# Six channel groups instead of three in a ConvFFN, with the down projection moved between the halves of the up projection

## The chip, the cores and the metric

The kernel runs on one core of one Trainium2 chip. A core has five engines that run side by side, each through its own instructions in order: TensorE (PE in the profile, its weight loads PEld) multiplies matrices into PSUM, VectorE (DVE) and ScalarE (ACT) work elementwise, GpSimd (POOL) does a few small things here, and SyncE (SP) issues the DMA transfers. PSUM has eight banks of 128 x 512 float32.

The metric is the device time of one execution in microseconds (us). The kernel before takes 1051.03 us, the median of three runs (1050.93 to 1052.33).

## The reference

Two layers of an encoder over 512 positions and 1024 channels, in float32. Each layer has a mixing part (a Fourier group and windowed attention, side by side, joined by `w_o`) and a ConvFFN. Cut to what matters:

```python
for l in range(2):
    h = rmsnorm(x, norm1[l])
    p = h @ w_in[l]                       # 1024 -> 512 Fourier | 512 q | 128 k | 128 v
    y_f = real(fft2(p[:, :512])) @ w_f + b_f
    y_a = windowed_gqa(rope(norm(q)), rope(norm(k)), v, sink)   # |i - j| <= 128
    x = x + concat(rmsnorm(y_f), rmsnorm(y_a)) @ w_o[l]
    h = rmsnorm(x, norm2[l])
    up = dwconv_centred(h @ w_up[l], conv_w[l], conv_b[l])      # 1024 -> 5632, 3 taps over positions
    gate, val = up[:, :2816], up[:, 2816:]
    x = x + (silu(gate) * val) @ w_down[l]                      # 2816 -> 1024
```

## The kernel before

**Layout.** Channels lie on the partitions, positions along the free axis: `x` is eight tiles of 128 x 512. The 2816 inner channels of the ConvFFN are 22 tiles of gate and 22 of value; a *pair* `fi` is gate tile `fi` and value tile `fi`.

**Precision.** Most products are made of two-part numbers. `split` (L100) makes the parts: ScalarE copies the rounded high part (`act`, L91, recorded as L92), VectorE subtracts it for the low part (`tt`, L94, recorded as L95). `mm3` (L116) multiplies in three passes, recorded as L122, L123 and L124. Weights arrive by DMA in a `wraw` tile of 128 x 1024 (three buffers, `wload`, L129) and are split into `whi` and `wlo` chunks of up to 512 columns (five buffers each, `wsplit`, L134).

**A pair with eight products** (`up_eight`, L428): for each of its two halves eight input tiles x three passes of 512 columns, 48 matmuls in all; four weight chunks are split; VectorE takes each half out of PSUM with the factor `rb2` of the norm.

**A pair with seven products** (`up_seven`, L440) treats the two halves and the two halves of the positions as a two-by-two block matrix and makes seven products of half the width in place of eight: 7 x 4 x 3 = 84 matmuls of 256 columns. In exchange VectorE forms four sums of weights, seven chunks are split, and the products are added up in more and shorter steps. It uses both `tp` banks of PSUM and one of the others. The combinations of the input that it needs (the T operands) are made once a layer by `seven_h` (L416), into sixteen tiles from `h_rooms` (L403). The fourth T product, which belongs to the second half alone, comes after the first half has been handed on. `SEVEN` (L37) names these pairs: four in the first layer, six in the second.

**After each half** `conv` (L476) applies three taps: one ScalarE instruction and two on VectorE (`stt`, L97, recorded as L98). After both, Silu, the product and a split give the pair's input `gu` to the down projection, in `slab` or `pT` tiles.

**Groups.** `GROUPS` (L36) cuts the 22 pairs into three groups of 8, 7 and 7. After a group's pairs come its eight down rows: for each of the eight tiles of `x`, one PSUM bank sums the group's products with `w_down`, and VectorE adds it to `x`. In the first layer's last group each row is followed by the square sums and the split of the next layer's norm (`norm_tile`, L335).

**Presplit.** During the first layer's ConvFFN, `presplit` (L153) splits the second layer's other weights into parts and stores them to HBM (`kept`), in 44 pieces. A piece is one ScalarE and one VectorE instruction and two stores; loads go into `m4` tiles, one job ahead. `next(ahead)` does a piece. Until now the first three `m4` tiles of `h_rooms` were also taken from those five buffers.

**Order.** The text of the program gives priorities; a scheduler with a model of the engines' times fixes each engine's order when the program is built. Instructions can therefore stand some way from where the text has them. At run time each engine keeps its order and waits where a result is late.

**First layer's Fourier stages.** In the first layer these run in plain float32 (L120). Each stage makes three PSUM tiles of even columns (`pe`) and one of odd ones (`po`), and `stage_out` (L714) copies them out with ScalarE.

The functions that the diff touches, and what calls them:

Of the kernel before, what the change touches and what calls it, by code (L numbers as in the profile page):

```python
# [12 lines left out]
ALU = mybir.AluOpType  # L13
# [22 lines left out]
GROUPS = [(0, 8), (8, 7), (15, 7)]  # L36
SEVEN = ((9, 12, 16, 19), (9, 11, 13, 16, 18, 20))  # L37


def encoder_kernel(tc, t):  # L40
# [445 lines left out]
    for l in range(L):  # L486
# [200 lines left out]
        for kk in range(KT // 2):  # L687
            if not l:
                wu = load_wu(l, kk)
            for k in (2 * kk, 2 * kk + 1):  # L690
# [7 lines left out]
                for m in range(3):  # L698
                    mm3(pee[m][:, :258], [z[:, m * P:(m + 1) * P] for z in h], we, st, sp_)
                for m in range(2):  # L700
                    mm3(poo[:, m * 256:(m + 1) * 256], [z[:, 256 + m * P:384 + m * P] for z in h], wo,
                        st and m == 0, sp_, skip_group_check=True)
# [11 lines left out]
        def stage_out(pe, po, scale, turned=False):  # L714

            tiles = []
            if not l:
                two = temp(1024, "slab")
            for m in range(2):
                a = halves(pair("slab")) if l else [two[:, m * 512:(m + 1) * 512]]  # L720
                put([z[:, :257] for z in a], pe[m][:, :257], scale)
                put([z[:, 257:] for z in a], po[:, m * 256 + 1:(m + 1) * 256], scale)
                tiles.append(a)
            return tiles, tail_out(pe, scale, turned)
# [3 lines left out]
        for stage in range(2):  # L728
            pe = [psum(), psum(), psum("sc")]
            po = psum()  # L730
            for m in range(3):
# [10 lines left out]
            for m in range(2):  # L742
                for i in range(2):
                    a, b = (ue, tabs) if stage == 0 else (tabs, ue)
                    mm3(po[:, m * 256:(m + 1) * 256], [z[:, 256 + m * P:384 + m * P] for z in a[i]],
                        [z[:, 256:512] for z in b[i]], m == 0 and i == 0, i == 1, skip_group_check=True)
# [77 lines left out]
        ts = []  # L824
        for f0, nf in GROUPS:
            gu = []
            for fi in range(f0, f0 + nf):
                ys_ = []
                n = fi - f0
# [129 lines left out]
```

## Time and profile before

| | |
|---|---|
| median of 3 runs | 1051.03 us |
| profiled execution, its own time | 1051.79 us |
| its span, first to last instruction | 1050.0 us |
| TensorE busy | 1032.8 us, 98% |
| VectorE busy | 797.3 us, 76% |
| ScalarE busy | 531.5 us, 51% |
| DMA | 140.1 MB, 41.4% of sixteen engines |
| mean granted TensorE clock | 0.998 |

A row of a timeline has the start in us from the beginning of the span, the duration in us, engine, line, operation, output <- inputs, shapes and how many instructions are merged; behind them, in brackets, how long the engine was idle before and what ended it. A row of a group has the count behind an x, then busy us and mean ns of one, then the idle time ahead of the group's instructions and what ended it. A row of a table by stage has the stretch and its length, then for PE, PEld, DVE, ACT and POOL the busy time with the number of instructions that touch it, then granted clock, DMA share and GB/s. A row of DMA issues has the count, KB each and the median us from issue to landing.

Durations of successive instructions overlap a little on PE, DVE and ACT, so busy time is the time in which at least one runs.

### The profile page before, as it was taken

The page shows a single profiled execution, that of the slowest core. Times are in us where ns is not written, and L with a number is a line of the kernel's source. Part 1 is how long each engine was busy: PE and PEld are TensorE (multiplying, and loading weights), DVE is VectorE, ACT ScalarE, POOL GpSimd, SP SyncE. Part 2 cuts the span into 40 slices and gives each one's busy share as a digit, 9 for nine tenths or more (in the row PEclk, how much of TensorE's full clock was granted, in tenths as well). Part 3 has the DMA queues.
Part 4 walks back from the last instruction along what each step waited for, and adds up shares of the span by engine and source line. Part 5 has one row for each costly group of instructions (what it writes and reads, how often), then busy time and mean ns, then how long its engine had stood idle before and what let it go on. Part 6 is the DMA issues. An engine that isn't in the chain of part 4 may idle for free.

```text
span 1050.0 us, 15349 instructions
## 1 busy us (share of the span) xinstructions
PE 1032.8 (98%) x5453; PEld 882.5 (84%) x5453; DVE 797.3 (76%) x1596; ACT 531.5 (51%) x1015; POOL 61.5 (6%) x142
## 2 busy tenths in 40 slices
PE   8998999999999999999999999999999999999998
PEld 8877778888788888888899877888888898889987
DVE  8778748697968997899829776387887698659972
ACT  5349735555425554465514686155553455326541
POOL 0004410000000000000000053000000000000000
PEclk9999999999999999999999999999999999999999
DMA  7232122354734459736766412423333233322332
GB/s 273 84 106 81 58 83 81 111 179 127 257 113 141 158 168 319 257 122 208 233 190 207 145 61 81 140 83 99 100 101 101 79 105 97 102 80 88 126 97 92
DMA packets 58177, 140.10 MB, mean 133 GB/s; under 512 B 6386, under 2 KB 17906, under 8 KB 58100
## 3 DMA queue, kind: packets, MB, share of 16 engines
q1 hardware_dynamic: 58100, 139.12, 41.4%
q8 instruction: 43, 0.70, 0.3%
q14 instruction: 34, 0.28, 0.1%
HBM read 116.02 MB, written 23.07 MB: 132 GB/s over the span
## 4 chain that ended last, share of the span: by engine, by line
PE 88%; DVE 7%; ACT 2%; issue 1%; DMA 1%; SPq 0%; POOL 0%; DVEq 0%; ACTq 0%; POOLq 0%
PE ps L124 27%; PE ps L122 27%; PE ps L123 27%; PE ps L668 2%; PE ps L661 2%; PE ps L649 1%; DVE act L95 1%; PE ps L120 1%; DVE tF L98 1%; DVE whi L95 1%; DVE tF L95 1%; PE ps L240 1%; PE ps L233 1%; ACT tA L92 1%; DVE slab L95 1%
## 5 line engine op out<-in xcount | busy, mean ns | idle before, releaser
L92 ACT ACTIVATE whi<-wraw 128x512 fp32r<-128x512 f32 (+1 forms) x306 | 187.1, 616 | 278.5 <-PE ps L124 239.1
L123 PE MATMUL ps<-act,wlo 128*128 128x512 f32 (+1 forms) x728 | 270.1, 372 | 0.0
L124 PE MATMUL ps<-act,whi 128*128 128x512 f32 (+1 forms) x728 | 270.1, 372 | 0.0
L122 PE MATMUL ps<-act,whi 128*128 128x512 f32 (+1 forms) x728 | 269.5, 372 | 0.0
L95 DVE TENSOR_TENSOR wlo<-wraw,whi 128x512 fp32r<-128x512 f32 (+1 forms) x314 | 207.2, 665 | 72.7 <-ACT whi L92 71.1
L123 PEld LDWEIGHTS ps<-act,wlo 128*128 128x128 f32 x728 | 137.1, 188 | 23.7
L124 PEld LDWEIGHTS ps<-act,whi 128*128 128x128 f32 x728 | 137.1, 188 | 23.2
L122 PEld LDWEIGHTS ps<-act,whi 128*128 128x128 f32 x728 | 136.9, 188 | 23.3
L98 DVE SCALAR_TENSOR_TENSOR tF<-tF,pb,tF 128x511 f32<-128x511 f32 x176 | 128.9, 744 | 3.1 <-ACT tF L92 2.5
L122 PE MATMUL ps<-slab,whi 128*128 128x512 f32 (+2 forms) x276 | 107.5, 390 | 0.8 <-ACT whi L92 0.8
L123 PE MATMUL ps<-slab,wlo 128*128 128x512 f32 (+2 forms) x276 | 105.7, 383 | 1.0 <-DVE wlo L95 1.0
L124 PE MATMUL ps<-slab,whi 128*128 128x512 f32 (+2 forms) x276 | 105.4, 384 | 0.4 <-DVE slab L95 0.3
L95 DVE TENSOR_TENSOR tF<-ps,rb 128x512 f32<-128x512 f32 (+1 forms) x94 | 60.5, 656 | 40.5 <-PE ps L124 27.2
L92 ACT ACTIVATE tF<-tF,pb 128x512 f32<-128x512 f32 x88 | 70.5, 808 | 12.6 <-DVE tF L95 9.9
L95 DVE TENSOR_TENSOR x<-x,ps 128x512 f32<-128x512 f32 (+1 forms) x65 | 43.2, 673 | 40.3 <-PE ps L124 40.0
L122 PE MATMUL ps<-pT,whi 128*128 128x512 f32 (+1 forms) x163 | 62.5, 385 | 0.0
L123 PE MATMUL ps<-pT,wlo 128*128 128x512 f32 (+1 forms) x163 | 62.4, 385 | 0.0
L122 PEld LDWEIGHTS ps<-slab,whi 128*128 128x128 f32 x276 | 52.3, 190 | 11.3 <-ACT whi L92 1.3
L124 PE MATMUL ps<-pT,whi 128*128 128x512 f32 (+1 forms) x163 | 61.5, 385 | 0.0
L124 PEld LDWEIGHTS ps<-slab,whi 128*128 128x128 f32 x276 | 52.1, 190 | 10.8 <-DVE slab L95 0.9
L123 PEld LDWEIGHTS ps<-slab,wlo 128*128 128x128 f32 x276 | 52.3, 189 | 10.5 <-DVE wlo L95 1.4
L653 DVE CUSTOM_DVE_ANT_0 tA<-ps,pb,nsink 128x256 f32<-128x256 f32 (+1 forms) x64 | 37.7, 603 | 14.5 <-PE ps L649 9.6
(202 smaller groups left out, 1659.8 us busy)
## 6 DMA issues: line engine op xcount, KB each, us to landing
wraw<-in_w_up_dram SPq DMA_DIRECT2D x88, 512.0 KB, 3.5
kept<-tA SPq DMA_DIRECT2D x56, 256.0 KB, 4.3
wraw<-in_w_down_dram SPq DMA_DIRECT2D x32, 448.0 KB, 3.4
wraw<-in_w_down_dram SPq DMA_DIRECT2D x16, 512.0 KB, 3.6
whi<-kept SPq DMA_DIRECT2D x28, 256.0 KB, 2.9
wlo<-kept SPq DMA_DIRECT2D x28, 256.0 KB, 3.6
kept<-tA SPq DMA_DIRECT2D x32, 192.0 KB, 2.8
wraw<-in_w_o_dram SPq DMA_DIRECT2D x8, 512.0 KB, 3.8
```

Source lines behind the costliest of these rows:

```text
L92: return nc.scalar.activation(out, in_, func, **kw)
L95: return (eng or nc.vector).tensor_tensor(out, a, b, op=op)
L98: return nc.vector.scalar_tensor_tensor(out=out, in0=a, scalar=s, in1=b, op0=op0, op1=op1)
L120: nc.tensor.matmul(out, a[0], b[0], start=start, stop=stop, **kw)
L122: nc.tensor.matmul(out, a[0], b[0], start=start, stop=False, **kw)
L123: nc.tensor.matmul(out, a[1], b[0], start=False, stop=False, **kw)
L124: nc.tensor.matmul(out, a[0], b[1], start=False, stop=stop, **kw)
L233: nc.tensor.matmul(pt[:, 2 * b:2 * b + 2], acc[:, b * P:(b + 1) * P], ones2, start=True, stop=True)
L240: nc.tensor.matmul(pt[:, b * P:(b + 1) * P], r[:, b:b + 1].to_broadcast([P, P]), ident, start=True, stop=True)
L653: nc.vector.tensor_tensor_reduce(out=pr[:, :n], in0=sc[:, :n], in1=mask[:, m0:m0 + n], scale=qs_scale[p][:, i, e:e + 1], scalar=nsink[:, l ...
L661: tr = nc.tensor.transpose(pp[:, j * P:(j + 1) * P], pr[:, j * P:(j + 1) * P], ident)
L668: pv = nc.tensor.matmul(py[64 * e:64 * e + 64, i0 * P:(i1 + 1) * P], vp[:, j, 64 * g:64 * g + 64], pT[:, half, e, b0:b0 + 2 * (i1 - i0) + ...
```

## The change

- The 22 pairs are cut into six groups of 4, 4, 4, 3, 3 and 4. A row of the down projection has three or four products instead of seven or eight, and there are 48 rows in a layer instead of 24.
- The down rows become a generator, `rows`. A group's rows are run one or two at a time after each half of the next group's pairs; two rows of the last group but one are kept for after the last pair; the last group's rows stand at the end. The weights of two rows come in one load with two runs in each partition.
- Seven products are used in 17 pairs instead of 10: seven in the first layer, ten in the second.
- The T operands for k = 0 and 1 are made ahead of the pairs, those for 2 and 3 after pairs 3 and 4. Their tiles no longer come from `m4`, but from the tables' and other tiles that are free in the ConvFFN.
- The pieces of presplit are handed out by pair (`PIECES`): one or two in the first seven pairs, then one beside a pair with seven products and three beside one with eight.
- The second layer's tables (`load_tables(1)`) are loaded ahead of the last rows, because their tiles now hold T operands until then; before, their text stood ahead of the pairs.
- In the first layer the Fourier stages make and copy out the odd columns ahead of the even ones.

The diff, cut to its core:

```diff
-GROUPS = [(0, 8), (8, 7), (15, 7)]
-SEVEN = ((9, 12, 16, 19), (9, 11, 13, 16, 18, 20))
+GROUPS = [(0, 4), (4, 4), (8, 4), (12, 3), (15, 3), (18, 4)]
+PIECES = [1, 1, 2, 1, 2, 2, 2] + [1, 3] * 7 + [3]
+SEVEN = ((7, 9, 11, 13, 15, 17, 19), (6, 8, 9, 11, 12, 14, 15, 17, 18, 20))
...
     def h_rooms():
-        for _ in range(3):
-            z = temp(1024, "m4", F32R)
-            yield from (z[:, :512], z[:, 512:])
-        for tag in ("v", "accA", "accF", "acc", "room"):
+        for tag in ("th0", "th1", "tl0", "tl1", "wt0", "wt1", "v", "accA", "accF", "acc", "room"):
...
-                for m in range(3):
-                    mm3(pee[m][:, :258], ...)
-                for m in range(2):
-                    mm3(poo[:, m * 256:(m + 1) * 256], ...)
+                for m in (0, 1, 2, 3, 4) if l else (3, 4, 0, 1, 2):
...
+            for m, odd in ((0, 0), (0, 1), (1, 0), (1, 1)) if l else ((0, 1), (1, 1), (0, 0), (1, 0)):
...
+            if not l:
+                odd()
             for m in range(3):
...
+            if l:
+                odd()
...
-        if l == 0:
-            tabs, alts, wt = load_tables(1)
+        room = h_rooms()
+        ts = [seven_h(k, h2, room) for k in range(2)]
...
+        def rows(f0, nf, gu):
+            last = f0 + nf == FT
             for m in range(KT):
-                next(ahead)
-                if f0 and m % 2:
-                    next(ahead)
-                w = wchunks(t["w_down"][l, m, :, f0 * P:(f0 + nf) * P], nf * P)
-                if f0 == 0 and m % 2:
-                    ts.append(seven_h(m // 2, h2, room))
+                if m % 2 == 0:
+                    raw = wtile()[:, :2 * nf * P].rearrange("p (m c) -> p m c", m=2)
+                    nc.sync.dma_start(raw, t["w_down"][l, m:m + 2, :, f0 * P:(f0 + nf) * P].rearrange("m p c -> p m c"))
+                w = wsplit(raw[:, m % 2, :])
...
+                yield
...
+        down = iter(())
+        for f0, nf in GROUPS:
+            gu = []
+            todo = KT - 2 if f0 + nf == FT else KT
+            halves_left = 2 * nf
+            for fi in range(f0, f0 + nf):
+                ys_ = []
+                for z, u in enumerate((up_seven if fi in SEVEN[l] else up_eight)(l, fi, h2, ts, rb2)):
+                    ys_.append(conv(l, fi + z * FT, u))
+                    for _ in range(-(-todo // halves_left)):
+                        next(down, None)
+                        todo -= 1
+                    halves_left -= 1
+                if fi in (3, 4):
+                    ts.append(seven_h(len(ts), h2, room))
+                for _ in range(PIECES[fi]):
+                    next(ahead)
...
+            for _ in down:
+                pass
+            down = rows(f0, nf, gu)
+        if l < L - 1:
+            acc = accum()
+            tabs, alts, wt = load_tables(1)
+        for m, _ in enumerate(down):
+            if m % 2:
+                next(ahead)
```

More of the change, by code (lines that the diff above doesn't have):

```diff
@@ L714, in stage_out @@
         def stage_out(pe, po, scale, turned=False):
-            tiles = []
             if not l:
                 two = temp(1024, "slab")
[L719 to L723, printed above, removed]
+            tiles = [halves(pair("slab")) if l else [two[:, m * 512:(m + 1) * 512]] for m in range(2)]
+            for m, odd in ((0, 0), (0, 1), (1, 0), (1, 1)) if l else ((0, 1), (1, 1), (0, 0), (1, 0)):
+                if odd:
+                    put([z[:, 257:] for z in tiles[m]], po[:, m * 256 + 1:(m + 1) * 256], scale)
+                else:
+                    put([z[:, :257] for z in tiles[m]], pe[m][:, :257], scale)
             return tiles, tail_out(pe, scale, turned)
@@ L730, in encoder_kernel, with odd @@
             po = psum()
+            def odd():
+                for m in range(2):
+                    for i in range(2):
+                        a, b = (ue, tabs) if stage == 0 else (tabs, ue)
+                        mm3(po[:, m * 256:(m + 1) * 256], [z[:, 256 + m * P:384 + m * P] for z in a[i]],
+                            [z[:, 256:512] for z in b[i]], m == 0 and i == 0, i == 1, skip_group_check=True)
+            if not l:
+                odd()
             for m in range(3):
@@ L741, in encoder_kernel @@
                         nc.tensor.matmul(o, alts[:, :P], z, start=False, stop=z is ut[-1])
[L742 to L746, printed above, removed]
+            if l:
+                odd()
             ue, ut = stage_out(pe, po, 1.0 if stage == 0 else 1.0 / 512.0)
@@ L862, in encoder_kernel @@
                     for k in range(nf):
-                        mm3(o, [z[:, (k % 4) * P:(k % 4 + 1) * P] for z in w[k // 4]],
-                            [gu[k][:, s, q0:q1] for s in range(2)], k == 0, k == nf - 1)
+                        mm3(o, [z[:, k * P:(k + 1) * P] for z in w], [gu[k][:, s, q0:q1] for s in range(2)],
+                            k == 0, k == nf - 1)
                     tt(x[m][:, q0:q1], x[m][:, q0:q1], o, ALU.add)
-                    if end:
+                    if last and l == L - 1:
                         nc.sync.dma_start(t["out"][m, :, q0:q1], x[m][:, q0:q1])
-                if l < L - 1 and f0 + nf == FT:
+                if last and l < L - 1:
                     nxt.append(norm_tile(m, g1[:, l + 1, :], acc))
-            xg = nxt
+                yield
[16 more added lines that the diff above has]
+                    next(ahead)
+                act(ys_[0], ys_[0], AF.Silu)
+                tt(ys_[0], ys_[0], ys_[1], ALU.mult)
+                if fi % 8 < 4:
+                    a = pair("slab")
+                else:
+                    if fi % 2 == 0:
+                        two = temp(2048, "pT", F32R).rearrange("p (n s q) -> p n s q", n=2, s=2)
+                    a = two[:, fi % 2]
+                split(a[:, 0, :], a[:, 1, :], ys_[0])
+                gu.append(a)
+            for _ in down:
[7 more added lines that the diff above has]
+                next(ahead)
+        xg = nxt
     for cm in reversed(ctxs):
```

38 lines of the change are left out of this document (8 added, 30 removed).

## The prediction

> **What bounds the kernel now.** I read the first page for the load of the engines and for the chain of work that ended last, then tables by stage, then single rows.
>
> ```profile
> span 1050.0 us, 15349 instructions
> PE 1032.8 (98%) x5453; PEld 882.5 (84%) x5453; DVE 797.3 (76%) x1596; ACT 531.5 (51%) x1015; POOL 61.5 (6%) x142
> PE 88%; DVE 7%; ACT 2%; issue 1%; DMA 1%; SPq 0%; POOL 0%; DVEq 0%; ACTq 0%; POOLq 0%
> ```
>
> A busy PE is not yet a PE at its pace, so the distance from one matmul's start to the next decides. PE's timeline around a pair with eight products and the first product of a pair with seven:
>
> ```profile
> 421.38 0.39 PE L122 MATMUL ps<-act,whi 128*128 128x512 f32 x1
> ...
> 432.26 0.28 PE L122 MATMUL ps<-act,whi 128*128 128x256 f32 x1
> ...
> 433.69 0.28 PE L122 MATMUL ps<-m,whi 128*128 128x256 f32 x1
> ```
>
> Between the first two starts lie the 48 matmuls of an eight-product pair: 10.88 us, 0.2267 us each. Between the last two lie the 12 of one of the seven products: 1.43 us, 0.119 us each. Next, the stages (PE busy, weight loads, DVE, ACT, POOL, then granted clock, DMA share, GB/s):
>
> ```profile
> 184.00:200.00 16.00, 16.00 (x80) 13.50 (x79) 6.03 (x11) 4.44 (x8) 1.01 (x1) 1.00 0.30 99
> 200.00:232.00 32.00, 32.00 (x143) 26.50 (x142) 31.65 (x53) 22.39 (x37) 0.00 (x0) 1.00 0.53 163
> 308.00:383.00 75.00, 75.00 (x411) 65.52 (x410) 65.18 (x116) 41.00 (x69) 0.00 (x0) 1.00 0.42 137
> 198.00:534.00 336.00, 334.13 (x1624) 282.74 (x1624) 283.95 (x495) 178.84 (x303) 2.13 (x6) 0.99 0.57 188
> 715.00:1047.00 332.00, 331.55 (x1717) 284.94 (x1715) 254.91 (x422) 154.78 (x257) 0.00 (x0) 1.00 0.31 97
> 282.87:290.05 7.18, 5.32 (x15) 3.70 (x14) 7.18 (x16) 2.02 (x4) 0.00 (x0) 0.76 0.95 301
> ```
>
> The two ConvFFN stages (198 to 534 and 715 to 1047) are 668 us, and TensorE sets their time. VectorE is next, with 85% in the first layer and 77% in the second. One hole is left, the last row: its 14 matmuls (15 with the one already running) should take 14 x 0.2267 = 3.17 us and took 7.18, so it costs 4.0. Its beginning:
>
> ```profile
> 279.67 0.52 ACT L92 ACTIVATE tA<-m 128x384 fp32r<-128x384 f32 x1 [3.26 <-DMA m<-in_w_qkv_dram]
> ...
> 284.31 0.50 PE L122 MATMUL ps<-slab,whi 128*128 128x512 f32 x1 [0.83 <-ACT whi L92]
> ...
> 285.11 1.89 DVE L95 TENSOR_TENSOR wlo<-wraw,whi 128x512 fp32r<-128x512 f32 x3
> ...
> 285.85 0.75 PE L123 MATMUL ps<-slab,wlo 128*128 128x512 f32 x1 [1.03 <-DVE wlo L95]
> 286.39 0.63 PE L124 MATMUL ps<-slab,whi 128*128 128x512 f32 x1
> ```
>
> ScalarE stood 3.26 us on a load for presplit, the weight splits queued behind it came late, VectorE was full (7.18 of 7.18), and PE starved. Afterwards the granted clock fell (0.76) and matmuls took 0.63 instead of 0.39: two waits of 1.9 us together were enough, so every new starvation costs more than its wait. The Trainium skill's page "TensorE: Matmul & The Clock Gate" (section on HAM oscillation) warns only of PE-idle gaps beyond about 3.4 us; by it this hole would have cost its waits alone, and the trace disagrees.
>
> The row with x3 gives VectorE's real pace: (1.89 - 0.684) / 2 = 0.60 per instruction, so back to back each costs its listed duration less 0.08.
>
> **The change part by part.**
>
> Seven for eight. Seven more pairs (three in the first layer, four in the second). One takes 7 x 1.43 = 10.01 us of PE instead of 10.88, saving 0.87; seven save **6.1 us**. Both PE stages run without waits, so this comes straight off the end as long as PE stays fed. The same page of the Trainium skill (section "Back-to-back issue gap", N/2.4 + 2.5 ns) gives as an estimate 84 x 0.109 = 9.2 against 48 x 0.216 = 10.4, or 8.3 for seven pairs, and the sum below would end 2.2 lower. This trace's steps are longer, the narrow ones most, so the sum goes by its rows.
>
> VectorE pays. The rows of the first ConvFFN, with shapes apart (count, busy, mean ns):
>
> ```profile
> L95 DVE TENSOR_TENSOR wlo<-wraw,whi 128x512 fp32r<-128x512 f32 x111 | 75.5, 684 | 11.4 <-ACT whi L92 10.9
> L98 DVE SCALAR_TENSOR_TENSOR tF<-tF,pb,tF 128x511 f32<-128x511 f32 x88 | 64.6, 744 | 1.6 <-ACT tF L92 1.4
> L95 DVE TENSOR_TENSOR tF<-ps,rb 128x512 f32<-128x512 f32 x36 | 24.6, 684 | 10.7 <-PE ps L124 8.2 <-ACT rb L92 2.4
> L95 DVE TENSOR_TENSOR x<-x,ps 128x512 f32<-128x512 f32 x23 | 15.3, 676 | 6.5 <-PE ps L124 6.5
> L95 DVE TENSOR_TENSOR tA<-m,tA 128x512 fp32r<-128x512 f32 x16 | 10.9, 688 | 7.4 <-ACT tA L92 6.7 <-DMA kept<-tA 0.7
> L95 DVE TENSOR_TENSOR tF<-act 128x512 f32<-128x512 f32 x8 | 5.3, 682 | 0.0
> L95 DVE TENSOR_TENSOR tF<-tF,ps 128x256 f32<-128x256 f32 x12 | 5.0, 415 | 0.0
> L95 DVE TENSOR_TENSOR sums<-wraw,wraw 128x512 f32<-128x512 f32 x4 | 2.8, 690 | 1.9 <-DMA wraw<-in_w_up_dram 1.9
> ```
>
> An eight-product pair costs VectorE 4 weight splits, 2 evictions, the product and the split of its result (8 x 0.60) and 4 convolution steps (4 x 0.66): 7.5 us. A seven-product pair has 7 splits, 4 weight sums, one wide eviction, product and split (14 x 0.60), 5 short ones (5 x 0.335) and the same 4 steps: 12.8. So each exchange adds 5.3. Six groups instead of three double the additions into x: 24 more in each layer, 24 x 0.60 = 14.5. The columns of w_down that are split stay the same. First layer: 284 + 14.5 + 3 x 5.3 = 314 of VectorE in 336 - 4.0 - 2.6 = 329 us, **95%**; second: 255 + 14.5 + 4 x 5.3 = 291 in 328, 88%.
>
> Down rows between the halves. A row of a group of four is 12 matmuls, 2.72 us of PE, and two VectorE instructions, 1.2 us. A seven-product pair with two rows is then PE 10.01 + 5.44 = 15.45 against VectorE 12.8 + 2.4 = 15.2; an eight-product pair 16.3 against 9.9. Presplit puts one piece (0.6) beside the former and three (1.8, a little more where a fold comes first) beside the latter. Each kind's worst neighbour is compensated by the next: over two slots 31.8 against 27.5. Nearest row: 308 to 383, where pairs without rows kept VectorE at 87% and cost PE nothing. I take stalls of **3.0 us** for both layers together; the bounds are 0 (those 75 us) and 32 (the second rival).
>
> The hole. Presplit's loads no longer share five buffers of one kind with the T operands, and its pieces no longer fall one to a down row with the T operands between. I take the whole **4.0** off; between 0 and 4.0. If it reappears it is inside the 3.0.
>
> T operands for k = 0, 1 go ahead of the pairs: 7.5 us of VectorE (two sums 1.2, four short 1.3, two splits 1.2, twice). From 184 to 200 VectorE is idle for 16 - 6.0 = 10, while the norm is reduced, so nothing. Without that cover 7.5 us join the backlog of 200 to 232, where VectorE is full already, up to 7.5 per layer.
>
> Loads and queues. w_down is still 48 loads of 512 or 384 KB, but each partition reads two runs. The nearest load with two runs a partition is w_in:
>
> ```profile
> wraw<-in_w_up_dram SPq DMA_DIRECT2D x88, 512.0 KB, 3.5
> wraw<-in_w_down_dram SPq DMA_DIRECT2D x16, 512.0 KB, 3.6
> wraw<-in_w_in_dram SPq DMA_DIRECT2D x4, 512.0 KB, 5.1
> ```
>
> So 0 to 1.5 us later, behind 5.4 us of rows: nothing. A pair's two loads and one w_down load now fill the three wraw buffers, and SP issues in order: a late release holds the load behind it and presplit's stores. Cover is the five whi/wlo buffers, five products of 1.43.
>
> First layer's Fourier stages, odd columns first; tables of the second layer loaded after the pairs. What they touch:
>
> ```profile
> 66.66 0.66 ACT L92 ACTIVATE slab<-ps 128x255 f32<-128x255 f32 x2 [0.58 <-PE ps L120]
> 67.10 0.48 PE L120 MATMUL ps<-slab,tab 128*128 128x258 f32 x1 [0.47 <-ACT slab L92]
> ...
> 89.02 1.14 ACT L92 ACTIVATE tab<-m 128x512 fp32r<-128x512 f32 x2
> 90.06 0.37 ACT L92 ACTIVATE tail<-ps 128x258 f32<-128x258 f32 x1
> ...
> 90.48 0.51 PE L649 MATMUL ps<-m,act 128*128 128x256 f32 x2 [0.36 <-ACT tail L92]
> ```
>
> The two odd evictions come last now and PE waits 0.47; ahead, they run under the even products: -0.5 (between -1 and +0.8, two evictions of 0.38 ahead of the even ones elsewhere). The table splits delay tail, 0.36: -0.4 (0 to -1). They join the last rows, where VectorE has 8 x 2.5 (two row instructions, two of the norm) + 3 x 0.6 + 4 x 0.6 = 24.4 for 21.8 of PE; the next projection covers those 2.6 us.
>
> Sum: 1051.79 (span 1050.0 and 1.8 around it) - 6.1 - 4.0 - 0.5 - 0.4 + 3.0 = 1043.8. The profiled execution lies 0.8 above the median of the runs, 1051.03: **1043** there.
>
> **The rivals.**
>
> Holes come back. Three presplit pieces in a row use up the load fetched one job ahead, so ScalarE stands on a load as at 279.67, with the weight splits behind it; there are eight such slots. For it: VectorE at 95% has little to catch up with. Against: five free buffers and whi/wlo in reserve. Two or three more holes of 4.0 give 1043 + 8 to 12 = 1051 to 1055.
>
> VectorE bounds the seven-product slots; this is the slower one. If it runs at listed durations (waits between instructions, each 0.08 longer), a slot costs 14 x 0.684 + 5 x 0.415 + 4 x 0.744 + 4 x 0.68 = 17.3, against 15.45. It decides once the five split buffers no longer carry the 1.9 into the next slot. Then 17 x 1.9 = 32, and 1051.0 - 11 + 32 = 1072. For it: 7.18 of 7.18 in the hole. Against: 200 to 232 full without a stall, and the eight-product slots' 5 us to spare.
>
> More than forecast: no new stalls, front end two us shorter, 1043 - 3 - 2 = 1038 or below.
>
> **How the numbers follow.** The forecast (1038 to 1049) has 0.60, holes 0.22, VectorE-bound slots 0.11, more than forecast 0.07. The range 1037 to 1055 leaves out the third and part of the fourth. No change here is within 0.2%, 2.1 us, about what runs can tell: 1048.9 to 1053.1. Faster: 0.60 + 0.07 + a fifth of the holes, 0.71; slower: 0.11 + a third of the holes, 0.18; within: 0.11.
>
> **What would show it.** Right: 512-wide steps of 0.227 and 256-wide of 0.119 through both ConvFFN stages, no granted clock under 1.00 there, VectorE near 95% and 88%, no PE wait at 66 us. Wrong: PE waits on wlo or whi inside the seven-product pairs, ACT waits on loads of presplit followed by a dip of the clock, or VectorE without idle time from the first row on. A slower 256-wide step than 0.119 would take the first term away.

## The result, and the profile after

The changed kernel takes 1045.76 us, the median of five runs (1045.22 to 1046.27); the kernel before took 1051.21 in the five runs beside them (1050.93 to 1052.33). The ratio is **0.9945, with a 95% interval of 0.9935 to 0.9956**: 5.5 us, half a per cent, faster. The forecast was 1043, within a range of 1037 to 1055: the sign and the range were right, and the forecast gain, 8.0 us, was 2.5 us larger than the measured one.

The first page of the changed kernel, engines and chain of work that ended last:

```profile
span 1043.8 us, 16032 instructions
PE 1025.7 (98%) x5696; PEld 888.4 (85%) x5696; DVE 857.2 (82%) x1721; ACT 546.9 (52%) x1057; POOL 61.1 (6%) x142
...
PE 90%; DVE 6%; ACT 2%; issue 1%; DMA 0%; POOL 0%; ACTq 0%; DVEq 0%; POOLq 0%
```

TensorE still sets the end. It has 243 more matmuls in the records and 7.1 us less busy time; VectorE has 60 us more. The two ConvFFN stages, and three stretches of the second one (columns as before: PE, PEld, DVE, ACT, POOL, granted clock, DMA share, GB/s):

```profile
198.00:534.00 336.00, 335.04 (x1762) 289.29 (x1762) 306.87 (x544) 185.01 (x322) 1.10 (x6) 1.00 0.59 191
715.00:1041.00 326.00, 323.37 (x1831) 284.24 (x1829) 279.85 (x472) 161.17 (x275) 0.00 (x0) 1.00 0.32 97
716.00:750.00 34.00, 34.00 (x152) 28.16 (x152) 32.43 (x55) 21.52 (x33) 0.00 (x0) 1.00 0.25 78
750.00:772.00 22.00, 20.23 (x117) 17.39 (x115) 21.90 (x39) 11.96 (x22) 0.00 (x0) 1.00 0.21 54
772.00:804.00 32.00, 32.00 (x182) 28.16 (x181) 27.91 (x47) 15.71 (x27) 0.00 (x0) 1.00 0.37 114
```

The granted clock is 1.00 in all of them. TensorE now loses time in the *second* layer, for which the view of the waits of before lists none: 20.23 busy of 22.00 from 750 to 772, exactly where VectorE has been nearly full since 716 (32.43 of 34, then 21.90 of 22). The view of the waits after, for 664 to 1050 (engine, what it waits for, then us in total, times, the longest):

```profile
PE ps L124 <- ACT tF L94: 1.0, 1, 1.0
PE ps L125 <- DVE wlo L97: 0.7, 2, 0.4
PE ps L124 <- ACT whi L94: 0.5, 1, 0.5
```

**Where the time went.** The first 25 us vary between executions by up to 1.5 us. So I cut each trace at three matmul groups that every version has: the column sums of the first norm, those of `accA` in the first layer's mixing part, and the same in the second layer. (The changed file is two lines longer above these places, so L233 before is L235 after, `act`, `tt` and `stt` move from L92, L95 and L98 to L94, L97 and L100, and the three lines of `mm3` from L122, L123 and L124 to L124, L125 and L126.) The markers in the timeline of before:

```profile
24.97 0.95 PE L233 MATMUL ps<-ones,acc 128*128 128x2 f32 x8
...
152.42 0.95 PE L233 MATMUL ps<-ones,acc 128*128 128x2 f32 x8
...
669.01 0.95 PE L233 MATMUL ps<-ones,acc 128*128 128x2 f32 x8
```

and of after:

```profile
25.17 0.95 PE L235 MATMUL ps<-ones,acc 128*128 128x2 f32 x8
...
150.59 0.95 PE L235 MATMUL ps<-ones,acc 128*128 128x2 f32 x8
...
663.39 0.95 PE L235 MATMUL ps<-ones,acc 128*128 128x2 f32 x8
```

That gives a *front* (first to second marker), a *first part* (second to third: the first layer's ConvFFN and the front of the second layer) and a *second part* (third marker to the end of the span: mainly the second ConvFFN). The runs in the next section are cut at the same rows:

| kernel | front | first part | second part | ratio to before, 95% interval |
|---|---|---|---|---|
| before | 127.45 | 516.59 | 381.0 | 1 |
| the change, 17 pairs with seven | 125.42 | 512.80 | 380.4 | 0.9945 (0.9935 to 0.9956) |
| six groups, ten pairs (e3) | 125.84 | 512.53 | 380.2 | 0.9945 (0.9933 to 0.9957) |
| 16 pairs, without pair 6 (e1) | 125.42 | 512.52 | 378.4 | 0.9930 (0.9917 to 0.9942) |
| three groups, 17 pairs (e2) | 127.43 | 521.77 | 388.8 | 1.0111 (1.0096 to 1.0126) |
| Fourier order of before (e4) | 126.56 | 512.61 | 380.4 | 0.9962 (0.9948 to 0.9976) |
| pair 21 for pair 6 (e5) | 125.43 | 512.70 | 379.8 | 0.9941 (0.9929 to 0.9954) |
| T sums on GpSimd (e6) | 125.81 | 517.66 | 380.7 | 1.0003 (0.9994 to 1.0012) |
| folds on GpSimd (e8) | 125.42 | 511.70 | 380.2 | 0.9939 (0.9927 to 0.9952) |
| pair 21 and folds on GpSimd (e9) | 125.41 | 511.70 | 379.2 | 0.9927 (0.9913 to 0.9940) |
| all T operands ahead (e10) | 125.82 | 511.76 | 379.7 | 0.9934 (0.9922 to 0.9947) |
| 16 pairs, folds on GpSimd (e11) | 125.52 | 511.66 | 378.4 | 0.9918 (0.9904 to 0.9931) |
| three T operands ahead, folds on GpSimd (e12) | 125.74 | 511.63 | 378.9 | 0.9919 (0.9905 to 0.9932) |

The intervals of many rows overlap; the segments of the profiled executions tell them apart, to about 0.4 us: that far they differ where nothing was edited (the fronts). In one case it is 0.6: the second parts of e5 and e9, whose second layers are the same text. All kernels compute the whole of the reference. The median of before lay between 1050.9 and 1052.05 in the different sets of runs, so kernels are compared by ratio and not by time.

Against before, the change gained 2.0 us in the front and 3.8 in the first part, and only 0.6 in the second, where four exchanged pairs should have brought 3.5.

### The profile page after: what moved, and what is told of

Same layout as the page of the kernel before. It is cut to its first block, busy times and chain, and to the rows that moved or that the text cites. A ratio compares the mean times of both kernels' runs of the same rounds, so it can differ in the third digit from the quotient of the medians.

```text
span 1043.8 us, 16032 instructions
## 1 busy us (share of the span) xinstructions
PE 1025.7 (98%) x5696; PEld 888.4 (85%) x5696; DVE 857.2 (82%) x1721; ACT 546.9 (52%) x1057; POOL 61.1 (6%) x142
## 4 chain that ended last, share of the span: by engine, by line
PE 90%; DVE 6%; ACT 2%; issue 1%; DMA 0%; POOL 0%; ACTq 0%; DVEq 0%; POOLq 0%
PE ps L124 27%; PE ps L126 27%; PE ps L125 27%; PE ps L122 3%; PE ps L667 2%; PE ps L660 2%; PE ps L648 1%; DVE tF L100 1%; DVE wlo L97 1%; ACT tA L94 1%; PE ps L242 1%; DVE tF L97 1%; PE ps L235 1%; DVE tA L652 1%; DVE x L97 0%
## 5 line engine op out<-in xcount | busy, mean ns | idle before, releaser
L94 ACT ACTIVATE whi<-wraw 128x512 fp32r<-128x512 f32 (+1 forms) x313 | 187.9, 614 | 230.9 <-PE ps L126 139.9
L125 PE MATMUL ps<-act,wlo 128*128 128x512 f32 (+1 forms) x700 | 250.1, 359 | 0.4 <-DVE wlo L97 0.4
L124 PE MATMUL ps<-act,whi 128*128 128x512 f32 (+1 forms) x700 | 250.5, 359 | 0.0
L126 PE MATMUL ps<-act,whi 128*128 128x512 f32 (+1 forms) x700 | 249.8, 359 | 0.0
L97 DVE TENSOR_TENSOR wlo<-wraw,whi 128x512 fp32r<-128x512 f32 (+1 forms) x321 | 210.0, 668 | 41.7 <-ACT whi L94 41.0
L125 PEld LDWEIGHTS ps<-act,wlo 128*128 128x128 f32 x700 | 132.0, 189 | 21.1 <-DVE wlo L97 1.1
L124 PEld LDWEIGHTS ps<-act,whi 128*128 128x128 f32 x700 | 132.0, 189 | 19.8
L126 PEld LDWEIGHTS ps<-act,whi 128*128 128x128 f32 x700 | 132.0, 189 | 19.2
L100 DVE SCALAR_TENSOR_TENSOR tF<-tF,pb,tF 128x511 f32<-128x511 f32 x176 | 130.2, 746 | 3.9 <-ACT tF L94 3.7
L124 PE MATMUL ps<-slab,whi 128*128 128x512 f32 (+2 forms) x274 | 105.8, 389 | 1.2 <-ACT whi L94 1.2
L125 PE MATMUL ps<-slab,wlo 128*128 128x512 f32 (+2 forms) x274 | 104.6, 382 | 0.0
L97 DVE TENSOR_TENSOR x<-x,ps 128x512 f32<-128x512 f32 (+1 forms) x113 | 75.2, 677 | 34.3 <-PE ps L126 34.0
L126 PE MATMUL ps<-slab,whi 128*128 128x512 f32 (+2 forms) x274 | 102.2, 383 | 0.3 <-DVE slab L97 0.3
L94 ACT ACTIVATE tF<-tF,pb 128x512 f32<-128x512 f32 x88 | 71.1, 811 | 29.7 <-DVE tF L97 28.0
L97 DVE TENSOR_TENSOR tF<-ps,rb 128x512 f32<-128x512 f32 (+1 forms) x87 | 54.4, 634 | 23.5 <-PE ps L126 12.2
L124 PE MATMUL ps<-room,whi 128*128 128x256 f32 x238 | 67.5, 283 | 1.1 <-ACT tF L94 1.0
L125 PE MATMUL ps<-room,wlo 128*128 128x256 f32 x238 | 67.2, 282 | 0.3 <-DVE wlo L97 0.3
L126 PE MATMUL ps<-room,whi 128*128 128x256 f32 x238 | 67.0, 282 | 0.0
L124 PE MATMUL ps<-pT,whi 128*128 128x512 f32 (+1 forms) x162 | 62.6, 388 | 0.0
L125 PE MATMUL ps<-pT,wlo 128*128 128x512 f32 (+1 forms) x162 | 62.6, 388 | 0.0
L126 PE MATMUL ps<-pT,whi 128*128 128x512 f32 (+1 forms) x162 | 61.7, 387 | 0.0
L124 PEld LDWEIGHTS ps<-slab,whi 128*128 128x128 f32 x274 | 51.5, 188 | 11.4 <-ACT whi L94 1.6
```

The source lines that it names most:

```text
L94: return nc.scalar.activation(out, in_, func, **kw)
L97: return (eng or nc.vector).tensor_tensor(out, a, b, op=op)
L100: return nc.vector.scalar_tensor_tensor(out=out, in0=a, scalar=s, in1=b, op0=op0, op1=op1)
L124: nc.tensor.matmul(out, a[0], b[0], start=start, stop=False, **kw)
L125: nc.tensor.matmul(out, a[1], b[0], start=False, stop=False, **kw)
L126: nc.tensor.matmul(out, a[0], b[1], start=False, stop=stop, **kw)
```

## The experiments

**e3: the six groups with the ten old pairs.** The theory: the gain of the seven exchanged pairs was largely eaten by waits.

```diff
-SEVEN = ((7, 9, 11, 13, 15, 17, 19), (6, 8, 9, 11, 12, 14, 15, 17, 18, 20))
+SEVEN = ((9, 12, 16, 19), (9, 11, 13, 16, 18, 20))
```

> The changed kernel with the ten pairs of seven products that the kernel before had. Theory: what is left of the change takes away the hole of 4.0 us and shortens the first layer's front by 1.8, and with less work on VectorE there are no new waits: 1051.2 - 5.8 = 1045.4, so the seven exchanged pairs brought nothing by themselves, having paid in waits what they saved. Rival: the new waits belong to the rows between the halves and stay: 1045.8 + 6.1 = 1051.9.

Measured: 0.9945 (0.9933 to 0.9957), the ratio of the change itself. The ConvFFN stages of this kernel:

```profile
198.00:534.00 336.00, 336.00 (x1653) 286.18 (x1652) 292.70 (x512) 178.87 (x304) 1.10 (x6) 1.00 0.58 191
715.00:1041.00 326.00, 325.33 (x1687) 280.09 (x1685) 261.07 (x428) 153.34 (x251) 0.00 (x0) 1.00 0.31 97
```

In the first stage TensorE is busy without a gap (336.00 of 336.00); the view of its waits is empty for both stages. The first part is 4.1 shorter than before, which is the size of the hole, and the second 0.8 shorter. So with ten pairs the six groups and their re-ordering alone give the whole 5.5 us, and **the seven exchanged pairs bring nothing net**: they save 7 x 0.87 = 6.1 of TensorE work, yet the first part is 0.27 and the second 0.2 longer than with ten. They give back 6.1 + 0.27 + 0.2 = 6.6 us; with the scatter of the segments, 6 to 7.

**e1: sixteen pairs, without pair 6 of the second layer.** The largest loss after the change lies in that pair. TensorE, as the timeline of after shows it:

```profile
764.47 0.38 PE L124 MATMUL ps<-room,whi 128*128 128x256 f32 x1 [0.97 <-ACT tF L94]
765.16 0.39 PE L125 MATMUL ps<-room,wlo 128*128 128x256 f32 x1 [0.30 <-DVE wlo L97]
...
769.99 0.50 PE L124 MATMUL ps<-slab,whi 128*128 128x512 f32 x1 [0.50 <-ACT whi L94]
```

and what VectorE and ScalarE did just then:

```profile
761.52 1.15 ACT L94 ACTIVATE whi<-wraw 128x512 fp32r<-128x512 f32 x2 [0.62 <-DVE wraw L97]
...
764.06 0.36 ACT L94 ACTIVATE tF<-ps 128x256 f32<-128x256 f32 x1
...
763.82 0.68 DVE L97 TENSOR_TENSOR sq<-tF,sq 128x512 fp32r<-128x512 f32 x1
764.42 1.28 DVE L97 TENSOR_TENSOR wlo<-wraw,whi 128x512 fp32r<-128x512 f32 x2
...
767.55 0.69 DVE L97 TENSOR_TENSOR wraw<-wraw,sums 128x512 f32<-128x512 f32 x1
768.27 0.63 ACT L94 ACTIVATE whi<-wraw 128x512 fp32r<-128x512 f32 x1 [0.90 <-DVE wraw L97]
```

VectorE is still making T operands (`sq`) while the pair needs its sums of weights. ScalarE waits 0.62 us for one (761.52), so what stands behind it in its order comes late, among it the instruction that takes a product of the pair out of PSUM (764.06), and TensorE waits 0.97 us for that (764.47). Then the same again: VectorE makes another sum late (767.55), ScalarE waits 0.90 us for it and splits it (768.27), the splits behind it are late, and TensorE waits 0.50 us for split weights (769.99). Counted from start to start of the matmuls against the usual steps (0.227 and 0.120), 2.7 us are lost between 763 and 770.

```diff
-SEVEN = (..., (6, 8, 9, 11, 12, 14, 15, 17, 18, 20))
+SEVEN = (..., (8, 9, 11, 12, 14, 15, 17, 18, 20))
```

> The changed kernel with eight products instead of seven in pair 6 of the second layer, its first such pair; nine stay in that layer. Theory: the 2.7 us lost at 763 to 770 come from VectorE, which starts the ConvFFN with a backlog (evictions wait for the norm), gets the T operands for k = 2 and 3 on top, and has not worked it off when pair 6 wants its weight sums. Then the waits go, 0.87 us of TensorE come back: 1045.8 - 2.7 + 0.9 = 1043.9, and the new first pair with seven products, 8, starts without a wait. Rival: the first pair with seven products always stumbles, whichever it is, because its two weight loads and the down weights share three buffers. Then the waits move to pair 8: 1045.8 + 0.9 = 1046.6.

Measured: 0.9930 (0.9917 to 0.9942), and the second part 378.4 instead of 380.4. The engines' load in the stretch with pair 6:

```profile
750.00:772.00 22.00, 22.00 (x99) 18.24 (x98) 20.98 (x37) 11.17 (x18) 0.00 (x0) 1.00 0.41 120
```

TensorE is busy for all of the 22 us. Dropping one seven-product pair costs 0.87 of work and gains 2.0, so the waits in and behind pair 6 were 2.9 us, nearly half of what the seven pairs lost. No wait of that size arose at the seven-product pairs that are left, pair 8 among them, so the rival (the first such pair always stumbles) is out; only one of 0.3 us is left in the whole stage.

**e2: three groups with the 17 pairs.** Undoes the interleaving of the down rows and keeps the number of seven-product pairs; the kernel before with other lists (7 in the first layer and 6 in the second are replaced by 21, since the T operands are only complete after the first group of eight):

```diff
-SEVEN = ((9, 12, 16, 19), (9, 11, 13, 16, 18, 20))
+SEVEN = ((9, 11, 13, 15, 17, 19, 21), (8, 9, 11, 12, 14, 15, 17, 18, 20, 21))
```

> The kernel before with 17 pairs of seven products and nothing else changed: three groups, down rows behind each group, (9, 11, 13, 15, 17, 19, 21) in the first layer and (8, 9, 11, 12, 14, 15, 17, 18, 20, 21) in the second. Theory: without rows between, five such pairs and two with eight products cost VectorE 5 x 12.8 + 2 x 7.5 = 79 us against 5 x 10.0 + 2 x 10.9 = 72 of TensorE, so each of the second layer's two groups loses 7 us, the first layer about 2: 1051.2 - 6.1 + 16 = 1061. Rival: VectorE's load was never the limit and the rows between are not needed for it: 1051.2 - 6.1 = 1045.

Measured: 1.0111 (1.0096 to 1.0126), 12 us slower than before. The price is as expected, its place and mechanism only in part: against the 0.87 a pair that should have been saved, the first layer loses 7.8 us by the segments, where about 2 had been expected, and the second 11.3, where 14 had been. Waits of TensorE from 715 on:

```profile
PE ps L123 <- DVE wlo L95: 3.2, 3, 1.6
PE ps L122 <- ACT tF L92: 2.7, 3, 1.5
PE ps L122 <- DVE tF L95: 1.6, 1, 1.6
```

and the engines' load in the two runs of pairs that hold most of them:

```profile
822.00:896.00 74.00, 70.75 (x476) 65.02 (x475) 65.91 (x115) 40.37 (x72) 0.00 (x0) 1.00 0.28 85
934.00:1020.00 86.00, 81.34 (x543) 74.43 (x542) 75.04 (x131) 45.00 (x82) 0.00 (x0) 1.00 0.28 86
```

VectorE has 8 of 74 and 11 of 86 us idle, so it is not simply full: TensorE waits for single results of the chain inside a pair (a product is evicted, combined, and its successor can start) and has no down row to fill the time. With three groups the step from ten to 17 pairs costs 12 us; with six it costs nothing (e3). That the rows between the halves are the part of the new arrangement that does it fits these waits, but was not tried alone.

**e4: the order of the Fourier columns put back.** Three places, even columns ahead of odd ones again in the first layer, all else as changed:

```diff
-                for m in (0, 1, 2, 3, 4) if l else (3, 4, 0, 1, 2):
+                for m in (0, 1, 2, 3, 4):
...
-            for m, odd in ((0, 0), (0, 1), (1, 0), (1, 1)) if l else ((0, 1), (1, 1), (0, 0), (1, 0)):
+            for m, odd in ((0, 0), (0, 1), (1, 0), (1, 1)):
...
-            if not l:
-                odd()
...
-            if l:
-                odd()
+            odd()
```

> The changed kernel with the even columns ahead of the odd ones again in the first layer's Fourier stages. Theory: the wait of 0.47 us at 66 us returns, and with the shift of what follows up to 1 us: 1046.3 to 1046.8, with the rest of the 1.8 us at the front coming from the table splits that no longer stand there. Rival: the whole 1.8 us comes from the order of the columns: 1047.6.

Measured: 0.9962 (0.9948 to 0.9976), between the two theories. The old wait is back, and the second marker comes later:

```profile
67.70 1.57 PE L122 MATMUL ps<-slab,tab 128*128 128x258 f32 x6 [0.47 <-ACT slab L94]
...
152.13 0.95 PE L235 MATMUL ps<-ones,acc 128*128 128x2 f32 x8
```

The front is 126.56 instead of 125.42 (125.41 to 125.84 in all the kernels with the new order): the order is worth 0.7 to 1.1, more than the wait of 0.47 that I could see. The remaining 0.9 of the front's 2.0 (127.45 to 126.56) belongs to the other edit there, the second layer's tables that are no longer split in that stretch, or to what the scheduler arranged differently with them; nothing tried separates these.

**e5: pair 21 in place of pair 6.** Keeps seventeen pairs and moves the one out of VectorE's backlog to the end, where VectorE has idle time.

```diff
-SEVEN = (..., (6, 8, 9, 11, 12, 14, 15, 17, 18, 20))
+SEVEN = (..., (8, 9, 11, 12, 14, 15, 17, 18, 20, 21))
```

> The changed kernel with the seven products of the second layer's pair 6 moved to pair 21, still 17 pairs. Theory (a backlog of VectorE early in the stage): the 2.7 us of waits at 763 to 770 go and nothing takes their place, since VectorE has 9 us to spare in the last 32 us of pairs (22.9 of 32 busy from 996 to 1028): 1045.8 - 2.7 = 1043.1, 0.9 below the run without pair 6. Rival (VectorE's sum over the stage counts, not the time): the waits turn up at pairs 20 and 21: 1045.8.

Measured: 0.9941 (0.9929 to 0.9954), a miss: the waits at 764 went, but the time is 1045.0 where 1043.1 had been expected, and the second part 379.8. The new waits are at the end; rows of TensorE, ScalarE and VectorE there:

```profile
1003.32 0.39 PE L125 MATMUL ps<-act,wlo 128*128 128x256 f32 x1 [0.72 <-DVE wlo L97]
...
1028.48 1.68 ACT L94 ACTIVATE whi<-wraw 128x512 fp32r<-128x512 f32 x3 [6.79 <-PE ps L126]
...
1028.48 2.48 DVE L97 TENSOR_TENSOR x<-x,ps 128x512 f32<-128x512 f32 x4 [6.06 <-PE ps L126]
1030.88 1.28 DVE L97 TENSOR_TENSOR wlo<-wraw,whi 128x512 fp32r<-128x512 f32 x2
...
1031.62 0.50 PE L125 MATMUL ps<-slab,wlo 128*128 128x512 f32 x1 [0.82 <-DVE wlo L97]
```

VectorE stands idle for 6.06 us and ScalarE for 6.79: the next instruction in the order of each waits for TensorE. Then ScalarE makes the high parts of the next weights at once, but VectorE does four additions into `x` ahead of their low parts, and TensorE waits 0.82 us for one of these. So the idle time was no reserve: the splits could not be made in it, and when they could, VectorE's order had other work first. The wait of 0.72 at 1003 comes out of a stretch that VectorE began late, after 1.15 us on a weight load (996.98), and in which it was full.

**e6: the sums of the T operands on GpSimd.** If VectorE's backlog is the cause, taking work off it should end the waits: 16 sums of 128 x 512 and the 32 short steps behind them go to the engine that is nearly idle.

```diff
-        tt(t13[:, LO], b1[:, HI], b1[:, LO], ALU.subtract)
+        tt(t13[:, LO], b1[:, HI], b1[:, LO], ALU.subtract, nc.gpsimd)
...
-            tt(b[i], f(h2[k + 4 * i][:, 0, :]), f(h2[k + 4 * i][:, 1, :]), ALU.add)
+            tt(b[i], f(h2[k + 4 * i][:, 0, :]), f(h2[k + 4 * i][:, 1, :]), ALU.add, nc.gpsimd)
```

> The changed kernel with the sums for the T operands made on GpSimd, which is idle in the ConvFFN, instead of VectorE (six instructions for each k; the splits stay). Theory: VectorE is relieved of 2 x 0.6 + 4 x 0.335 = 2.5 us for each k, two of them in the backlog ahead of pair 6, so the waits at 763 to 770 shrink by half or more: 1044.0 to 1044.5. Rival: GpSimd is slower at these (0.59 us for a 128x256 instruction with one input in this trace) and the operands for k = 3 come too late for pair 6, so that the waits stay or grow: 1046 to 1048.

Measured: 1.0003 (0.9994 to 1.0012), all of the gain lost, nearly all of it in the first part (517.66). GpSimd needs 1.71 us for a sum; worse, VectorE slows while it runs. From the groups of e6, those of the sums in the whole span, then one of VectorE from 175 to 200, where the first ConvFFN begins:

```profile
L97 POOL TENSOR_TENSOR tF<-act 128x512 f32<-128x512 f32 x16 | 27.3, 1712 | 98.5 <-DVE tF L97 52.8 <-DVE act L100 41.4 <-DVE slab L97 2.5
...
L97 DVE TENSOR_TENSOR x<-x,tF 128x512 f32<-128x512 f32 x2 | 3.0, 1496 | 0.0
```

The load of its engines there:

```profile
175.00:190.00 15.00, 13.06 (x57) 10.07 (x55) 15.00 (x13) 6.01 (x11) 13.77 (x11) 1.00 0.24 72
```

The same group in the same stretch of the changed kernel:

```profile
L97 DVE TENSOR_TENSOR x<-x,tF 128x512 f32<-128x512 f32 x2 | 1.4, 679 | 0.0
```

The listed time of one such addition goes from 0.679 to 1.496 us, and with GpSimd busy 13.77 of 15 us VectorE gets through only 13 instructions (28 in the changed kernel). What the norm and the first splits need came late, so TensorE lost its time at the start of the stage and in its first pairs. The waits that the run was to cure did shrink: in the second layer's pair 6 this one is left,

```profile
776.19 0.38 PE L124 MATMUL ps<-act,whi 128*128 128x256 f32 x1 [0.47 <-ACT tF L94]
```

and by the steps 0.7 us are lost there instead of 2.7, as the theory said. But 2.2 us more are lost ahead of it, between 700 and 711, so the second part is no shorter (380.7); and since TensorE comes to the pair later too, the run does not show which of the two made the waits shrink.

**e8: the folds of presplit on GpSimd.** Less work and not in a hurry: the sums and differences by which presplit folds twelve of its pieces (the folds of one layer's Fourier weights), in the stage where VectorE is at 91%.

```diff
-        tt(dst[..., 1:256], src[..., 1:256], src[..., 511:256:-1], ALU.add)
+        tt(dst[..., 1:256], src[..., 1:256], src[..., 511:256:-1], ALU.add, eng)
...
-        tt(w[:, :256], raw[:, :256], raw[:, 256:512], ALU.add)
+        tt(w[:, :256], raw[:, :256], raw[:, 256:512], ALU.add, eng)
```

> The changed kernel with the folds of presplit on GpSimd instead of VectorE (twelve pieces of the first layer, three instructions each). Theory: the 1.4 us lost at 372 in the first layer come from VectorE, where two folds of presplit stand between the splits and sums of pair 13; without them the waits go: 1045.8 - 1.4 = 1044.4, the second layer's stay. Rival: they come from the four rows beside pair 12 and not from the folds: 1045.8.

Measured: 0.9939 (0.9927 to 0.9952), which does not differ from the change by its interval; the first part, the only one that the edit touches, is 511.70 instead of 512.80. Of these 1.1 us, 0.4 arise only after 617, in the second layer's mixing part, which the edit does not touch; e3 and e10, with the folds on VectorE, are as short there. So 0.7 is what the edit brings in the stage itself. The change's largest wait of the first layer, in pair 13 right behind three pieces with folds, and the same place in e8, each from the timeline. After:

```profile
373.02 0.49 PE L124 MATMUL ps<-slab,whi 128*128 128x512 f32 x1 [0.65 <-ACT whi L94]
```

and e8:

```profile
372.72 0.39 PE L125 MATMUL ps<-act,wlo 128*128 128x256 f32 x1 [0.17 <-DVE wlo L97]
```

The main part of the folds among the groups of GpSimd in e8:

```profile
L97 POOL TENSOR_TENSOR tA<-m 128x255 f32<-128x255 f32 (+1 forms) x24 | 24.5, 1041 | 24.5 <-DVE tA L97 24.5
```

By the steps the loss there falls from 1.4 to 0.4 us, while one at 520 grows from 0.3 to 0.5. So the folds in a slot of three pieces were most of that wait.

**e9: e5 and e8 together**, to see whether the two edits add up.

> Both: seven products in pair 21 instead of 6, and the folds of presplit on GpSimd. Theory: the effects add, since they lie in different layers: 1045.8 - 2.7 - 1.4 = 1041.7. Rival: as for the two alone, 1043.1 to 1045.8.

Measured: 0.9927 (0.9913 to 0.9940), better than either alone, but by intervals that overlap, and 1043.5 rather than the 1041.7 of the theory: the first part gains what e8 gained, and the second (379.2; 379.8 with the same second layer in e5) gains 1.2 of the 2.7 expected, so pair 21 keeps part of its price.

**e10: all T operands ahead of the pairs.** Moves the backlog to where VectorE had idle time.

```diff
-        ts = [seven_h(k, h2, room) for k in range(2)]
+        ts = [seven_h(k, h2, room) for k in range(4)]
...
-                if fi in (3, 4):
-                    ts.append(seven_h(len(ts), h2, room))
```

> The changed kernel with all four sets of T operands made ahead of the pairs, none after pairs 3 and 4; still 17 pairs of seven products. Theory (a backlog of VectorE early in the stage): of the 7.5 us for k = 2 and 3 up to 7.4 fit into what VectorE still has idle around the reduction of the norm (28.6 of 36 us busy from 680 to 716), so the backlog is shorter by that at pair 6 and the 2.7 us of waits at 763 to 770 go or shrink to under 1: 1043.1 to 1044.1. Rival: the backlog only starts earlier, because the last input tiles come too late for the idle time, and the waits stay or turn up ahead of the first rows: 1045.8 or more.

Measured: 0.9934 (0.9922 to 0.9947). The engines' load by stage:

```profile
680.00:716.00 36.00, 36.00 (x164) 29.94 (x163) 34.38 (x65) 17.14 (x30) 2.39 (x1) 1.00 0.32 100
750.00:772.00 22.00, 22.00 (x127) 19.42 (x126) 19.73 (x33) 11.50 (x20) 0.00 (x0) 1.00 0.30 96
```

and a new wait in TensorE's timeline:

```profile
719.14 0.50 PE L124 MATMUL ps<-act,whi 128*128 128x512 f32 x1 [1.80 <-DVE tF L97]
```

The waits of pair 6 are gone (22.00 of 22.00), *with* pair 6 still of seven products. TensorE comes to that pair 1.8 us later, but VectorE has 2.3 us idle there (19.73 of 22.00), so its backlog is gone. That supports the cause by another route than e1: it was the T operands for k = 2 and 3, still being made. But 1.80 us of wait arose at the start of the stage, where VectorE now takes the first evictions late. The 7.5 us of VectorE work fit before the pairs only in part. So theory and rival both came true in part. The first part is shorter too, 511.76 instead of 512.80: a wait of 0.4 at 270 is gone and the second layer's mixing part is 0.4 shorter, as in e8, while the loss in pair 13 stays (1.3 by the steps).

**e11: sixteen pairs and the folds on GpSimd** (e1 and e8), the version that these runs pointed to.

> Eight products in the second layer's pair 6 (16 pairs with seven) and the folds of presplit on GpSimd. Theory: the two gains lie in different layers and add: 1045.8 - 1.8 - 1.1 = 1042.9, and the second layer's stage has no wait over 0.5 us left but the one at 960. Rival: GpSimd's instructions slow VectorE's beside them, so that the folds' gain of 1.1 does not carry over: 1044.0.

Measured: 0.9918 (0.9904 to 0.9931), 1042.60 us against 1051.91 beside it; the profiled execution's span is 1040.8 us. Its interval lies below that of the change (0.9935 to 0.9956): with one seven-product pair *less* it is faster than both kernels.

**e12: seventeen pairs, three T operands ahead, the fourth after pair 4, folds on GpSimd.** Asks whether the seventeenth pair pays once its wait is cured as far as possible.

> 17 pairs with seven products as in the changed kernel, three sets of T operands ahead of the pairs and the fourth after pair 4, and the folds of presplit on GpSimd. Theory: half of what was moved by making all four ahead, 3.8 us, still fits the idle time around the norm, so the wait of 1.8 us that all four brought at 719 stays away, and what is left of the backlog no longer reaches pair 6: 1045.8 - 2.7 - 1.1 = 1042.0, the best so far. Rival: either wait comes back in part, 1043 to 1044, and 16 pairs (1042.6) are as good as 17.

Measured: 0.9919 (0.9905 to 0.9932), the same as e11. The wait at the start of the second layer's stage is still there, but shorter than in e10: 0.71 us at 718.42, and 1.1 us lost by the steps around it; another 0.4 is lost at 768. The second part is 378.9 against 378.4 in e11, within the scatter: what the seventeenth pair saves, 0.87, does not make up for these losses. Sixteen pairs are as good as seventeen here, as the rival said.

## Why the prediction was right, and where its sum was wrong

The sum against the segments (spans: before 1050.0, after 1043.8):

| term | forecast | measured | from |
|---|---|---|---|
| seven pairs, TensorE work | -6.1 | -6.1 | steps unchanged, below |
| the hole | -4.0 | -4.1 | first part, before to e3 |
| Fourier order and table splits | -0.9 | -2.0 | front, before to after |
| second part with ten pairs | 0 | -0.8 | before to e3 (381.0 to 380.2) |
| ahead of the first marker | 0 | +0.2 | 24.97 to 25.17 |
| new stalls | +3.0 | +6.6 | e3 to after, plus the 6.1 |
| sum | -8.0 | -6.2 | |

The total came close in part by luck. The exchange of pairs, with its stalls, was forecast at -6.1 + 3.0 = -3.1 and measured +0.5: by itself it brought nothing. The other terms were forecast at -4.9 and measured -6.7, which hid about half of that miss.

**The steps of TensorE: right.** A product of 12 narrow matmuls, and three wide ones, of after:

```profile
794.85 0.39 PE L124 MATMUL ps<-slab,whi 128*128 128x512 f32 x1
...
795.53 0.39 PE L124 MATMUL ps<-slab,whi 128*128 128x512 f32 x1
...
796.21 0.28 PE L124 MATMUL ps<-act,whi 128*128 128x256 f32 x1
...
797.65 0.28 PE L124 MATMUL ps<-room,whi 128*128 128x256 f32 x1
```

From 794.85 to 795.53 are three steps of 0.227, from 796.21 to 797.65 twelve of 0.120. So the 0.87 a pair stands. The formula of the Trainium skill's page "TensorE: Matmul & The Clock Gate" (section "Back-to-back issue gap", where it is given for an isolated matmul: 0.216 and 0.109), by which the sum would have ended 2.2 lower, disagrees with these rows.

**The hole: right in size.** It is absent with six groups (after, e3) and present with three (e2, 17 pairs). Which of its two causes named in the prediction mattered, the shared `m4` buffers or the spacing of the pieces, was not tried apart.

**The front: right in sign, 1.1 too small.** The order of the columns was costed at the one wait of 0.47 in the quoted rows; e4 measures 0.7 to 1.1. The table splits, with what the scheduler moved with them, took 0.9 and not 0.4.

**The new stalls: the step that failed.** The term was 3.0 and measured 6.6; its bounds, 0 and 32, held it. The reasoning was that a seven-product pair's excess of VectorE work is made good by the next slot, with the stretch of pairs without rows as the nearest row; that balance is right for the second layer's pairs 8 to 20, which lost 0.6 in all. It did not count what VectorE had still to do when the seven-product pairs begin: the T operands for k = 2 and 3, put after pairs 3 and 4, on top of the backlog from the stage's start. In the second layer, where there is no presplit but pair 6 comes first, 2.9 of the 6.6 lie there (e1; e10 by the other route). In the first layer the three pieces with folds in a slot (1.4 at 372, of which e8 took 0.9) are the largest single place; the prediction had them as "a little more where a fold comes first". One of the signs that it named for being wrong, waits of TensorE on split weights inside pairs with seven products, is what these rows show. Single smaller waits make up 1.3 more (0.4 at 270, 0.3 at 520, 0.6 at 961). The remaining 1.0 is spread over delays too small to be named. One sum of the prediction has a slip without effect: 8 x 2.5 + 3 x 0.6 + 4 x 0.6 for the last rows is 24.2 and not 24.4.

**VectorE's load: total nearly right, wrong in its place.** 306.87 of 336 (91%) and 279.85 of 326 (86%) against 95% and 88%: part of the T operands lies ahead of the windows, as forecast, and the sum had counted all of them inside. But an average of 86% hid 54.3 of 56 us from 716 to 772, where the wait arose.

**The cover of the T operands ahead: right for two, not for four.** For k = 0 and 1 no wait arose at the start of the stage; e10 puts all four there, and 1.80 us appear.

**Loads: a little off, without effect.** The prediction allowed 0 to 1.5 us more for loads with two runs a partition. In the DMA issues of after:

```profile
wraw<-in_w_down_dram SPq DMA_DIRECT2D x32, 512.0 KB, 4.0
```

0.4 more than the 3.6 before for the same size; no wait for them is among TensorE's.

**The rivals.** Holes come back: no wait of TensorE after the change goes back to a load of presplit, and the clock does not fall. VectorE bounds all the seven-product slots: no, TensorE is busy 335.04 of 336 and 323.37 of 326; but its mechanism, VectorE behind at a point where the split buffers no longer carry it, is what happened at pair 6 of the second layer and, weaker, at pair 13 of the first. More than forecast: the front did come out 1.1 shorter than forecast, about half of the two us that this rival asks for, while the stalls went the other way.

## What to carry to other kernels

Cost an exchange of TensorE work for VectorE work slot by slot, from the first slot on, with all that VectorE has already queued there; an average load of 86% says nothing about the one slot that is late. Ask of the last few such exchanges whether they pay at all: here ten pairs were as good as seventeen, and sixteen with the folds moved off VectorE were better than either. And an engine's idle time is reserve only if the late work can be done in it and the engine's order lets it come first.

## What the runs showed of the hardware

**Elementwise work on GpSimd slows VectorE.** In e6 a sum of 128 x 512 took 1.71 us on GpSimd against 0.68 on VectorE, and VectorE's own 128 x 512 instructions that overlapped one took 1.10 us in the mean (45 of them, up to 1.78) instead of 0.685; in e8 1.00 us (30 of them). "One" is here any of the moved sums, steps or folds. Only those with both inputs in SBUF are slower: the eight of the 45 that read PSUM took 0.68 us and the other 37 1.20; in e8 four took 0.68 and 26 1.04. The Trainium skill's page "SBUF — State Buffer" (section "Who interferes with whom") says that a VectorE instruction with two SBUF inputs contends with a GpSimd instruction that reads SBUF, and calls the port pair that they share an exclusive lock. These runs agree as to which instructions are held up; whether for whole instructions, the listed durations do not resolve. Folds of 24.5 us on GpSimd, spread over a stage, still paid (e8: 0.7 us in the stage, by the segments); 63 us of sums, much of them at the busy start of a stage, cost the whole gain (e6).

**The clock does not fall after every starvation.** The prediction took from the hole (waits of 0.83 and 1.03 within 3 us, granted clock 0.76) that each new one costs more than its wait. After the change, 0.97 and 0.30 at 764 left the clock at 1.00, and so did one wait of 1.80 in e10 and one of 1.58 in e2:

```profile
841.21 0.39 PE L122 MATMUL ps<-m,whi 128*128 128x256 f32 x1 [1.58 <-DVE tF L95]
```

The same hole in e2 (waits of 0.6 and 1.0) has a granted clock of 0.83 from 280 to 290; in its table by stretches, behind the 1.58 and around the hole:

```profile
841.00:845.00 4.00, 3.79 (x31) 3.79 (x32) 3.63 (x7) 2.61 (x6) 0.00 (x0) 1.00 0.81 237
...
280.00:290.00 10.00, 8.33 (x29) 6.18 (x28) 10.00 (x21) 4.57 (x10) 0.00 (x0) 0.83 0.95 295
```

The Trainium skill's page "TensorE: Matmul & The Clock Gate" (section on HAM oscillation) asks for no idle gap beyond about 3.4 us: the 1.80 and the 1.58 agree with it, the two dips do not. In before the granted clock is 0.50 from 285.93 to 289.34 and 1.00 again behind it, so the dip lasted 3.4 us; that, and not only the waits, is where the hole's 4.0 us come from. What separates these cases is open: the two that dipped waited 1.7 and 1.9 us in all, the three that did not 1.3, 1.58 and 1.80.
